# One layer of a hybrid streaming encoder: the adaLN modulation's products issued two loads at a time, in all four column groups

## The chip, the cores and the metric

One core of a Trainium2 chip runs the whole kernel. The metric is device time in microseconds of one execution. The core has a matrix engine (TensorE, PE; its weight loads are listed as PEld), a vector engine (VectorE, DVE), a scalar engine (ScalarE, ACT), GpSimd (POOL) and SyncE (SP), which issues most of the DMAs. Matrix results go to PSUM, everything else lies in SBUF.

## The reference, cut to what matters

Two groups of tokens (256 of a prompt, 32 of a sample, 288 in all) go through one layer of width 2048. Each of the two sequences has a vector c, and the layer begins with the modulation:

```python
(shift1, scale1, gate1, shift2, scale2, gate2) = silu(c) @ w_mod[l] + b_mod[l]
h = RMSNorm(x) * (1 + scale1) + shift1
P = h @ w_in[l]
...
x = x + gate1 * (merged @ w_out[l])
x = x + gate2 * SqReLU_MLP(RMSNorm(x) * (1 + scale2) + shift2)
```

w_mod is 2048 x 12288 in float32: six parts of 2048 columns, 16.8 MB each. Between h and merged lie three mixers (a gated recurrence, a state-space scan, a gated token mix); w_in, w_branch, w_out, w_up and w_down are the other large weights. All of it is read once from memory and has only 288 tokens (2 columns, for the modulation) to work on.

## The kernel before, in words

**Large products** (`product`, `product_part`, `product_group`). Weights arrive in tiles `raw` of 128 x 1024 float32 (512 KB), are split into a high and a low half by ACT (`whi`, L395) and DVE (`wlo`, L396), and three float32r matmuls of 288 columns for each 128 x 128 block add up the product (L382 to L384 in the first products, L413 to L415 later). There are six `raw` buffers, three `whi` and three `wlo`.

**The modulation.** silu(c) of the two sequences, padded to 32 columns, is the stationary operand `cT` (128 x 32 per block k of the contraction, 16 blocks). The moving operand is a block of w_mod. As the stationary operand has 32 columns only, a product fills one of the four 32-column groups of the array; its output goes to rows 32 cg to 32 cg + 31 of the PSUM tile `modps`, where cg is the group. The tiles of w_mod share the six `raw` buffers with the other weights.

Three generators make it, and `mods` chains them; one `next` is a step, which is one load and what follows it:
- `mod_stream` (L234 to L256) makes parts 0 and 1 (shift1, scale1), which the first products need. Units are 256 columns (the first eight) or 512 (the last four). A load has nk = 4 blocks of 256 columns or nk = 2 blocks of 512; block k goes to group k % 4, so a load of 256 columns has one product for each of the four groups, and a load of 512 columns has products for two of them. A product is the matmul at L246. After the last load of a unit, ACT copies the PSUM tile (L251), and `mod_flush` adds up the four groups with a selector (L317).
- `mod_parts` (L292 to L307) makes part 2 (gate1) in halves of 1024 columns. A load is one block k of 1024 columns, cut into four quarters of 256 columns, one for each group (L298).
- `mod_part_ve` makes parts 4, 3 and 5 on the vector engine; it isn't touched.

**The order.** The first products go through the contraction in the six parts `KG`, because h becomes known block by block; the loop over `KG` calls `mod_steps` 1.5 times for each weight tile (`MODR`) until parts 0 and 1 are done, and then 0.2 times (`RS`). In `product_group` the rate `mod_rate` is 0.2 at first and 0.4 from branch A on. Instructions are written in this order and a planner at build time, which runs a model of the time, arranges each engine's queue by priority: `tc.high_priority(offset=PRIO)` moves an instruction up by 2500 places, as is done with all loads and casts. The matmuls of the modulation have their ordinary place. The hardware then runs each queue in its order, with waits on semaphores; a buffer is taken again when all that read it are done.

Of the kernel before, what the change touches and what calls it, by code (L numbers as in the profile page):

```python
# [16 lines left out]
P = 128  # L17
D = 2048
NB = D // P            # blocks of the model width
SEQ, DEC = 256, 32  # L20
T = SEQ + DEC          # prompt tokens, then sample tokens
TX = T + 2             # and the shift of each sequence
# [4 lines left out]
CVB = 12               # blocks of the conv channels  # L27
# [9 lines left out]
def tile_step(ctx, tc, io, outs):  # L37
    nc = tc.nc
    V, S, G, TE = nc.vector, nc.scalar, nc.gpsimd, nc.tensor
# [7 lines left out]
    PRIO = 2500  # L47
    # the later parts of the modulation in their order, and those summed on the vector engine
    MOD_PARTS = (2, 4, 3, 5)
    MOD_VE = (4, 3, 5)  # L50
    # modulation steps per weight tile: in the first products, before, in and after branch A, in branch B,
    # in the output projection, in the MLP
    MODR, RS, RA, RB, RD, RW, RC = 1.5, 0.2, 0.4, 0.3, 0.5, 0.5, 0.25
    # buffers
    RAW, WHI, WLO = 6, 3, 3
    MTAG = ("raw", RAW)
    EVB = 6
    BLK = 34
    TMPB = 10
    # column pairs by which a branch's gates run ahead of its outputs  # L60
# [35 lines left out]
    # ------------------------------------------------------------------  # L96
    # constants
    # ------------------------------------------------------------------
# [7 lines left out]
    # triangular mask [s, t]: 1 where s <= t  # L106
# [3 lines left out]
    # scan resets at the chunk starts  # L110
# [4 lines left out]
    # selector that adds the four column groups of the modulation products  # L115
# [7 lines left out]
    def level_mask(pool, L):  # L123
        """mask [s, t] of the pairs that level L joins: one L-block, s in its first half, t in its second."""
        m = t1("lvm")
        if L == 1:
            V.tensor_copy(out=m, in_=ident)
        else:
            h = L // 2
            n = P // L  # L130
            G.memset(m, 1.0)
            if n > 1:
                G.affine_select(out=m, in_=m, pattern=[[-L, n], [0, L]], compare_op=ALU.is_ge,
                                fill=0.0, base=0, channel_multiplier=1)
            G.affine_select(out=m, in_=m, pattern=[[L, n], [0, L]] if n > 1 else [[0, L]], compare_op=ALU.is_ge,
                            fill=0.0, base=h - 1, channel_multiplier=-1)
            G.affine_select(out=m, in_=m, pattern=[[0, n], [1, L]] if n > 1 else [[1, L]], compare_op=ALU.is_ge,
                            fill=0.0, base=-h, channel_multiplier=0)
        # its 32-blocks next to each other
        mc = t1("lvm")[:, 0:32]  # L140
        V.tensor_reduce(out=mc, in_=m.rearrange("p (g t) -> p t g", g=4), axis=mybir.AxisListType.X, op=ALU.add)
        mu = pool.tile([P, 32], U8, name=f"lvm{L}")
        V.tensor_copy(out=mu, in_=mc)
        lv_masks[L] = mu

    # ------------------------------------------------------------------
    # parameters: rows to columns
    # ------------------------------------------------------------------
    # silu(c), feature-major, padded with zero columns
# [6 lines left out]
    with tc.high_priority(offset=2 * PRIO):  # L156
        ps = aux()
# [4 lines left out]
    # ones in one column of a sequence  # L162
# [5 lines left out]
    # x token-major, three blocks at a time (the sample's two)  # L168
# [59 lines left out]
    # ------------------------------------------------------------------  # L228
    # modulation: silu(c) @ w_mod + b_mod, as [feature, part*16+block, sequence]
    # ------------------------------------------------------------------  # L230
# [3 lines left out]
    def mod_stream(units):  # L234
        """256 or 512 columns at a time; a step is one load and its products."""
        for u, (c0, w) in enumerate(units):
            ps = paux.tile([P, 512], F32, tag="modps", name=nm("modps"), bufs=2)
            nk = 1024 // w
            for q in range(NB // nk):
# [3 lines left out]
                for i in range(nk):  # L243
                    k = nk * q + i
                    cg = k % 4
                    TE.matmul(ps[32 * cg:32 * cg + 32, 0:w], cT[:, k, :], raw[:, i, :],  # L246
                              start=k < 4, stop=k >= 12)
# [9 lines left out]

    def mod_part_ve(part):
        """A part in quarters of 512 columns, summed on the vector engine but for the sum over the partitions;
        a step is two blocks of the contraction."""  # L260
# [22 lines left out]
    def mod_parts(parts):  # L283
        """A part in halves of 1024 columns, a quarter of them in each group of 32 rows; a step is one block
        of the contraction."""
        for part in parts:
# [3 lines left out]
            for half in range(2):  # L290
                ps = paux.tile([P, 512], F32, tag="modps", name=nm("modps"), bufs=2)
                c0 = part * D + half * 1024  # L292
                for k in range(NB):
                    with tc.high_priority(offset=PRIO):
                        raw = wpool.tile([P, 1024], F32, tag=MTAG[0], name=nm("mraw"), bufs=MTAG[1])
                        nc.sync.dma_start(out=raw, in_=wm[:, k, c0:c0 + 1024])
                    for cg in range(4):
                        TE.matmul(ps[32 * cg:32 * cg + 32, 0:256], cT[:, k, :], raw[:, cg * 256:(cg + 1) * 256],  # L298
                                  start=k == 0, stop=k == NB - 1)
                    if k == 1:  # L300
                        mod_flush()
                    yield
# [8 lines left out]
    def mod_flush():  # L311
        """To feature-major, and adds the bias."""
# [26 lines left out]
    # the first products go through the contraction in these parts, as the modulation arrives  # L339
# [11 lines left out]
    def mod_drain(last):  # L351
        """All of the modulation up to a part."""
# [4 lines left out]
    # ------------------------------------------------------------------  # L357
    # streamed products: out^T[f, t] = sum_d w[d, f] a[d, t], three float32r passes
    # ------------------------------------------------------------------
    def product(w2d, col0, ncols, ahi, alo, evac, row0=0, n=T):  # L360
        """Groups of 256 columns; evac(j, psum) for each 128-column block."""
# [8 lines left out]
    def product_part(wv, cols, k0, nk, ahi, alo, accs, first):  # L370
        """nk blocks of the sum over d for sets of 256 columns, added to accs."""
# [50 lines left out]
    # ------------------------------------------------------------------  # L422
    # x feature-major, rms statistics, h = rmsnorm(x) (1 + scale1) + shift1
    # ------------------------------------------------------------------
# [55 lines left out]
    # ------------------------------------------------------------------  # L480
    # mixers
    # ------------------------------------------------------------------
# [3 lines left out]
    def setup_a():  # L486
# [3 lines left out]
        # lower bound of the forget gate: cumsum(softmax) - first, over the depth axis (one layer)  # L490
# [14 lines left out]
    bA, kA, qA, gA, vA = {}, {}, {}, {}, {}  # L505

    def evac_f(h0, pts):
        """log f, its running sum, and 1 - f of two heads; exponentials and logarithms from one table set."""
# [25 lines left out]
    def to_tokens(dst, src):  # L534
        """[feature, token] to [token, chunk, feature]."""
# [22 lines left out]
    def mixer_a(h):  # L558
# [4 lines left out]
        for L in (1, 2, 4, 8, 16, 32, 64, 128):  # L563
# [33 lines left out]
            # the joined pairs are whole squares  # L597
# [36 lines left out]
        # per-head rms norm  # L634
# [8 lines left out]
    def inv_rms(sq, scale):  # L643
        """1 / sqrt(scale * (sum of sq over its partitions) + eps), on all partitions."""
# [56 lines left out]
    def pair_rows(out, j, rows):  # L701
        """Rows 2 j and 2 j + 1 of a [16, n] tile, each on 64 partitions."""
# [4 lines left out]
    # time steps  # L707
# [18 lines left out]
    def do_dt():  # L726
# [26 lines left out]
        # token-major: [token, chunk, (dt | acum | dt * decay)]  # L753
# [8 lines left out]
        # exp(acum_last) on all partitions, for the second prompt chunk and the sample  # L762
# [7 lines left out]
        # acum in three parts of f32r each, 32 rows apart, and a selector that adds a head's three  # L770
# [16 lines left out]
    def mixer_b_cb(g):  # L787
        """C B^T of a group, causal, as [s, t]; B token-major."""
# [12 lines left out]
    def mixer_b(j):  # L801
        """Heads 2 j and 2 j + 1."""
# [10 lines left out]
        # x * dt and x * dt * decay, token-major  # L813
# [78 lines left out]
    def branch(kk, first, y, last=False):  # L892
        """gate_k * (y_k @ w_branch_k), added up; a step is 256 columns of it."""
# [101 lines left out]
    # ------------------------------------------------------------------  # L995
    # order of the work
    # ------------------------------------------------------------------
# [62 lines left out]
    # the last three tokens of each sequence are the new conv states  # L1060
# [14 lines left out]
    # The shift goes through the product in columns of its own, and 1 / rms comes after the product.  # L1075
# [55 lines left out]
    def final(j):  # L1131
        """Block j of the output: its squares, and times final_g."""
# [8 lines left out]
    def turn(j):  # L1141
        """Block j token-major."""
# [112 lines left out]
```

## Time and profile before

| | |
|---|---|
| device time, median of 3 runs | 2113.21 us (2109.93 to 2116.8) |
| the profiled execution: its span, which is the time the profile has for it | 2112.9 us |
| PE busy | 2079.8 us (98%) |
| PEld busy | 1966.6 us (93%) |
| DVE, ACT, POOL busy | 1442.7, 985.7, 156.6 us |
| read and written in memory | 405.04 MB, 4.62 MB |

The profile has one execution. An instruction is listed with the line that issued it, its engine and what it writes and reads (`out<-in`); groups of equal instructions are listed with their count, busy time and mean. A matmul's end is modelled and matmuls overlap, so what PE needs for a piece of work is read from start to start. A float32 matmul shows as two records, a float32r matmul as one. The chain of work that ended last is PE for 96% of the span.

### The profile page before, as it was taken

To read this page: it belongs to the slowest core of one execution; us is meant where nothing else is said; L and a number is where in the kernel's file an instruction comes from. 1 tells how busy PE (TensorE), PEld (TensorE's weight loads), DVE (VectorE), ACT (ScalarE), POOL (GpSimd) and SP (SyncE) were. 2 spreads that over 40 slices of the span, in tenths; PEclk is the share of its full clock that TensorE was granted. 3 is DMA by queue.
4 is the path that set the end of the run, shared out by engine and by line. 5 is a ranking of instruction groups with operands and counts; after the bars stand their busy time and mean duration, and the time that the engine had idled before them with its cause. 6 is when DMAs were issued, how large, how long until landed. Compare 5 with 4: busy or idle time off the path is not lost.

```text
span 2112.9 us, 40517 instructions
## 1 busy us (share of the span) xinstructions
PE 2079.8 (98%) x16336; PEld 1966.6 (93%) x16336; DVE 1442.7 (68%) x2546; ACT 985.7 (47%) x1553; POOL 156.6 (7%) x278
## 2 busy tenths in 40 slices
PE   6999999999999999999999999999999999999997
PEld 4777998988999999999999999999999999999997
DVE  2565666756578887787988998766774455555565
ACT  4432584655555545545444445433453344334443
POOL 2020112000000110110100110000000000000010
PEclk9999999999999999999999999999999999999999
DMA  9987655456566565666877777666664555555542
GB/s 295 295 263 238 217 150 163 144 183 179 181 204 196 172 192 183 191 183 182 268 245 221 221 226 229 201 206 203 199 210 160 169 160 166 164 169 161 167 156 91
DMA packets 364844, 412.31 MB, mean 195 GB/s; under 512 B 14777, under 2 KB 325457, under 8 KB 364657
## 3 DMA queue, kind: packets, MB, share of 16 engines
q1 hardware_dynamic: 360784, 403.97, 61.3%
q0 software_dynamic: 3008, 4.58, 0.7%
q8 instruction: 128, 2.10, 0.4%
q10 hardware_dynamic: 864, 1.18, 0.2%
q14 instruction: 60, 0.48, 0.1%
HBM read 405.04 MB, written 4.62 MB: 194 GB/s over the span
## 4 chain that ended last, share of the span: by engine, by line
PE 96%; DVE 1%; ACT 1%; DMA 1%; POOL 0%; issue 0%; SPq 0%; POOLq 0%; ACTq 0%; DVEq 0%
PE mm L413 26%; PE mm L415 26%; PE mm L414 26%; PE mm L382 3%; PE mm L383 3%; PE mm L384 3%; PE modps L246 2%; PE modps L298 1%; PE aux L185 1%; PE aux L856 1%; PE aux L584 1%; PE modps L317 0%; PE aux L538 0%; PE modps L328 0%; PE aux L631 0%; PE aux L601 0%
## 5 line engine op out<-in xcount | busy, mean ns | idle before, releaser
L395 ACT CAST whi<-raw 128x1024 fp32r<-128x1024 f32 x568 | 595.4, 1049 | 911.3 <-PE mm L414 701.5
L396 DVE TENSOR_TENSOR wlo<-raw,whi 128x1024 fp32r<-128x1024 f32 x568 | 695.0, 1224 | 453.8 <-ACT whi L395 451.2
L413 PE MATMUL mm<-hlo,whi 128*128 128x288 f32 x1408 | 421.3, 300 | 0.0
L414 PE MATMUL mm<-hhi,whi 128*128 128x288 f32 x1408 | 419.2, 299 | 0.0
L415 PE MATMUL mm<-hhi,wlo 128*128 128x288 f32 x1408 | 413.2, 299 | 0.0
L414 PE MATMUL mm<-h2hi,whi 128*128 128x290 f32 x1024 | 303.9, 297 | 0.0
L413 PE MATMUL mm<-h2lo,whi 128*128 128x290 f32 x1024 | 303.5, 297 | 0.0
L415 PE MATMUL mm<-uhi,wlo 128*128 128x288 f32 x1024 | 303.3, 296 | 0.0
L415 PE MATMUL mm<-h2hi,wlo 128*128 128x290 f32 x1024 | 302.8, 297 | 0.0
L413 PE MATMUL mm<-ulo,whi 128*128 128x288 f32 x1024 | 301.2, 294 | 0.0
L414 PE MATMUL mm<-uhi,whi 128*128 128x288 f32 x1024 | 301.1, 294 | 0.0
L274 DVE SCALAR_TENSOR_TENSOR macc<-mraw,cT,macc 128x512 f32<-128x512 f32 x360 | 259.2, 745 | 24.5 <-DMA mraw<-in_w_mod_dram 24.2
L413 PEld LDWEIGHTS mm<-hlo,whi 128*128 128x128 f32 x1408 | 265.5, 189 | 9.1 <-issue 6.8
L414 PEld LDWEIGHTS mm<-hhi,whi 128*128 128x128 f32 x1408 | 265.8, 189 | 2.4 <-issue 0.9
L415 PEld LDWEIGHTS mm<-hhi,wlo 128*128 128x128 f32 x1408 | 263.3, 189 | 3.3 <-issue 1.0
L413 PEld LDWEIGHTS mm<-h2lo,whi 128*128 128x128 f32 x1024 | 194.0, 189 | 0.5 <-ACT r L1162 0.2
L415 PEld LDWEIGHTS mm<-h2hi,wlo 128*128 128x128 f32 x1024 | 193.9, 190 | 0.2 <-issue 0.2
L414 PEld LDWEIGHTS mm<-h2hi,whi 128*128 128x128 f32 x1024 | 193.9, 189 | 0.1
L413 PEld LDWEIGHTS mm<-ulo,whi 128*128 128x128 f32 x1024 | 193.0, 188 | 0.4 <-issue 0.4
L414 PEld LDWEIGHTS mm<-uhi,whi 128*128 128x128 f32 x1024 | 192.6, 188 | 0.0
L415 PEld LDWEIGHTS mm<-uhi,wlo 128*128 128x128 f32 x1024 | 192.2, 188 | 0.1
L382 PE MATMUL mm<-hlo,whi 128*128 128x288 f32 x448 | 138.6, 309 | 0.4 <-DVE hlo L472 0.4
(398 smaller groups left out, 3085.4 us busy)
## 6 DMA issues: line engine op xcount, KB each, us to landing
raw<-in_w_in_dram SPq DMA_DIRECT2D x204, 512.0 KB, 3.9
mraw<-in_w_mod_dram SPq DMA_DIRECT2D x128, 512.0 KB, 4.1
raw<-in_w_up_dram SPq DMA_DIRECT2D x128, 512.0 KB, 3.8
raw<-in_w_down_dram SPq DMA_DIRECT2D x128, 512.0 KB, 3.4
raw<-in_w_mod_dram SPq DMA_DIRECT2D x64, 512.0 KB, 5.0
raw<-in_w_branch_dram SPq DMA_DIRECT2D x48, 512.0 KB, 4.2
raw<-in_w_out_dram SPq DMA_DIRECT2D x32, 512.0 KB, 4.6
raw<-in_w_in_dram SPq DMA_DIRECT2D x56, 256.0 KB, 4.7
```

What stands on the lines that cost most here:

```text
L185: TE.transpose(ps[:, t0:t0 + n], xrow[c, i][:, k * P:(k + 1) * P], ident[0:n, 0:n])
L246: TE.matmul(ps[32 * cg:32 * cg + 32, 0:w], cT[:, k, :], raw[:, i, :], start=k < 4, stop=k >= 12)
L274: V.scalar_tensor_tensor(out=acc[s], in0=raw[:, i], scalar=cs, in1=acc[s], op0=ALU.mult, op1=ALU.add)
L298: TE.matmul(ps[32 * cg:32 * cg + 32, 0:256], cT[:, k, :], raw[:, cg * 256:(cg + 1) * 256], start=k == 0, stop=k == NB - 1)
L382: TE.matmul(pt, whi[:, i, cs], alo[k], start=i == 0, stop=False)
L383: TE.matmul(pt, whi[:, i, cs], ahi[k], start=False, stop=False)
L384: TE.matmul(pt, wlo[:, i, cs], ahi[k], start=False, stop=i == nk - 1)
L395: S.copy(out=whi, in_=raw)
L396: V.tensor_sub(out=wlo, in0=raw, in1=whi)
L413: TE.matmul(pts[b], whi[:, i, cs], alo[k], start=k == 0, stop=False)
L414: TE.matmul(pts[b], whi[:, i, cs], ahi[k], start=False, stop=False)
L415: TE.matmul(pts[b], wlo[:, i, cs], ahi[k], start=False, stop=k == nk - 1)
```

## The change

Products of the modulation aren't issued at each load any more. `mod_stream` keeps them in `held` and issues them at every second load, with a new function `mod_cols`: for 512 columns that is four products, one for each group, and for 256 columns eight products, two for each group. `mod_parts` does the same with `MODB = 2` loads, eight products. The newest load's products go first (`reversed`), so that the first instruction waits for the later load; the others are made to follow it in PE's queue by `together`, which puts an edge from the first product to each of the others and raises their priority. `start` and `stop` (the first and the last product that adds to a PSUM region) follow the new order. All else in the diff is comments that are left out and line numbers that move.

```diff
+    MODB = 2
...
     def mod_stream(units):
         for u, (c0, w) in enumerate(units):
             ps = paux.tile([P, 512], F32, tag="modps", name=nm("modps"), bufs=2)
             nk = 1024 // w
+            held = []
             for q in range(NB // nk):
                 with tc.high_priority(offset=PRIO):
                     raw = wpool.tile([P, nk, w], F32, tag="raw", name=nm("raw"), bufs=RAW)
                     nc.sync.dma_start(out=raw, in_=wm[:, nk * q:nk * (q + 1), c0:c0 + w])
-                for i in range(nk):
-                    k = nk * q + i
-                    cg = k % 4
-                    TE.matmul(ps[32 * cg:32 * cg + 32, 0:w], cT[:, k, :], raw[:, i, :],
-                              start=k < 4, stop=k >= 12)
+                held += [(nk * q + i, raw[:, i, :]) for i in range(nk)]
+                if q % 2:
+                    mod_cols(ps, held, w)
+                    held = []
...
+    def together(works):
+        first = works[0]()
+        with tc.issue_after(first.ins), tc.high_priority(offset=PRIO):
+            for work in works[1:]:
+                work()
+
+    def mod_cols(ps, held, w):
+        works, begun = [], set()
+        for k, r in reversed(held):
+            cg = k % 4
+            works.append(partial(TE.matmul, ps[32 * cg:32 * cg + 32, 0:w], cT[:, k, :], r,
+                                 start=held[0][0] == 0 and cg not in begun, stop=k == held[0][0] + cg and held[-1][0] == NB - 1))
+            begun.add(cg)
+        together(works)
...
     def mod_parts(parts):
...
+                held = []
                 for k in range(NB):
                     with tc.high_priority(offset=PRIO):
                         raw = wpool.tile([P, 1024], F32, tag=MTAG[0], name=nm("mraw"), bufs=MTAG[1])
                         nc.sync.dma_start(out=raw, in_=wm[:, k, c0:c0 + 1024])
-                    for cg in range(4):
-                        TE.matmul(ps[32 * cg:32 * cg + 32, 0:256], cT[:, k, :], raw[:, cg * 256:(cg + 1) * 256],
-                                  start=k == 0, stop=k == NB - 1)
+                    held.append((k, raw))
+                    if len(held) == MODB:
+                        together([partial(TE.matmul, ps[32 * cg:32 * cg + 32, 0:256], cT[:, k1, :],
+                                          r[:, cg * 256:(cg + 1) * 256], start=k < MODB and k1 == k,
+                                          stop=k == NB - 1 and k1 == held[0][0])
+                                  for k1, r in reversed(held) for cg in range(4)])
+                        held = []
```

## Rows read from the trace of the kernel before

**Rows 1.** The page, busy time of each engine.
```profile
PE 2079.8 (98%) x16336; PEld 1966.6 (93%) x16336; DVE 1442.7 (68%) x2546; ACT 985.7 (47%) x1553; POOL 156.6 (7%) x278
```

**Rows 2.** The page, busy tenths of PE in 40 equal slices.
```profile
PE   6999999999999999999999999999999999999997
```

**Rows 3.** Busy time by stretch: instructions in brackets, granted clock, DMA share, GB/s.
```profile
12.00:40.00 28.00, 22.93 (x140) 12.66 (x132) 7.05 (x17) 13.28 (x44) 6.60 (x20) 1.00 1.05 352
40.00:105.00 65.00, 65.00 (x529) 51.60 (x528) 34.96 (x63) 29.73 (x55) 0.00 (x0) 1.00 0.89 283
105.00:222.00 117.00, 117.00 (x788) 88.47 (x788) 71.02 (x151) 34.62 (x46) 11.88 (x21) 1.00 0.80 253
222.00:620.00 398.00, 393.43 (x3510) 359.75 (x3507) 264.21 (x596) 231.61 (x380) 45.96 (x88) 0.99 0.58 173
```

**Rows 4.** Timeline of PE around one visit: start, busy, instruction, records.
```profile
233.34 0.30 PE L383 MATMUL mm<-hhi,whi 128*128 128x288 f32 x1
233.48 0.29 PE L384 MATMUL mm<-hhi,wlo 128*128 128x288 f32 x1
233.70 0.64 PE L298 MATMUL modps<-mraw,cT 128*32 128x256 f32 x8
234.27 0.40 PE L382 MATMUL mm<-hlo,whi 128*128 128x288 f32 x1
234.51 0.30 PE L383 MATMUL mm<-hhi,whi 128*128 128x288 f32 x1
```

**Rows 5.** Timeline of PE, three visits of other sizes.
```profile
84.48 1.07 PE L246 MATMUL modps<-raw,cT 128*32 128x256 f32 x16
...
104.79 1.05 PE L246 MATMUL modps<-raw,cT 128*32 128x512 f32 x2
...
114.24 1.06 PE L246 MATMUL modps<-raw,cT 128*32 128x512 f32 x8
```

**Rows 6.** Timeline of PEld, the weight loads of the visit at 114.24.
```profile
114.24 0.16 PEld L246 LDWEIGHTS modps<-raw,cT 128*32 128x32 f32 x8 [0.16 <-issue]
```

**Rows 7.** Groups by shape on PE, 40 to 222 us: records, busy us, mean ns.
```profile
L246 PE MATMUL modps<-raw,cT 128*32 128x512 f32 x128 | 30.1, 604 | 0.0
L246 PE MATMUL modps<-raw,cT 128*32 128x256 f32 x168 | 15.0, 388 | 0.0
```

**Rows 8.** Timeline of PE, the first and last visits of each kind.
```profile
40.84 0.64 PE L246 MATMUL modps<-raw,cT 128*32 128x256 f32 x8
...
102.64 1.06 PE L246 MATMUL modps<-raw,cT 128*32 128x256 f32 x6
...
217.04 0.62 PE L246 MATMUL modps<-raw,cT 128*32 128x512 f32 x2
217.05 0.63 PE L298 MATMUL modps<-mraw,cT 128*32 128x256 f32 x4
...
607.90 0.64 PE L298 MATMUL modps<-mraw,cT 128*32 128x256 f32 x8
```

**Rows 9.** Groups by shape on PE, 217 to 620 us.
```profile
L298 PE MATMUL modps<-mraw,cT 128*32 128x256 f32 x256 | 23.8, 400 | 1.7 <-DMA mraw<-in_w_mod_dram 1.7
```

**Rows 10.** Timeline of PE at the start, two visits of L246.
```profile
18.61 1.08 PE L246 MATMUL modps<-raw,cT 128*32 128x256 f32 x8 [0.56 <-DMA raw<-in_w_mod_dram]
...
27.79 1.94 PE L246 MATMUL modps<-raw,cT 128*32 128x256 f32 x16
```

**Rows 11.** Waits before L246 (us, times): whole span first, then two of 40 to 222.
```profile
  DMA raw<-in_w_mod_dram: 12.4, 7
...
  issue: 6.6, 37
  PE mm L383: 0.3, 2
```

**Rows 12.** Modulation loads on the page (KB, us to landing); ACT's wait, 40 to 222.
```profile
raw<-in_w_mod_dram SPq DMA_DIRECT2D x64, 512.0 KB, 5.0
...
ACT whi L395 <- DMA raw<-in_w_in_dram: 35.2, 10, 6.0
```

More of the change, by code (lines that the diff above doesn't have):

```diff
@@ L1 @@
 from contextlib import ExitStack
+from functools import partial
 from itertools import chain
```

## The prediction

> **What bounds the kernel now.** I read the page's busy times first. TensorE (PE) is busy 98% of the span [rows 1], and its line of slices shows the one hole, in the first slice [rows 2]. The table by stretch says the same where the change acts: PE is busy 65.00 of 65.00 us from 40 to 105, 117.00 of 117.00 from 105 to 222, and 393.43 of 398.00 from 222 to 620 [rows 3]. A busy PE can still be slow, so I looked at single starts in the timeline: ordinary matmuls follow each other at 0.13 to 0.14 us (233.34 to 233.48 in [rows 4]), without holes. So from 40 us on, a microsecond that PE no longer needs comes off the end, as long as the loads keep up. They nearly don't: the DMA share is 0.89 and then 0.80 in the first two stretches, where the modulation's weights arrive, and only 0.58 after [rows 3].
>
> **How a modulation visit is priced.** Each fp32 product shows as two matmul records. I call a run of modulation records between other matmuls a visit. Around the visit at 233.70 [rows 4] the matmul before starts at 233.48 and the second one after at 234.51: 1.03 us in which two ordinary spacings would have used 0.27. The visit costs 0.76 us where its row shows 0.64 busy, so cost is busy time plus 0.12.
>
> The records then show what a visit's length depends on [rows 5]:
> - two records of 512 columns (one product, one column group): busy 1.05;
> - eight records of 512 columns (four products, four groups): busy 1.06;
> - eight of 256 columns (four groups, once): 0.64 [rows 4];
> - sixteen of 256 columns (four groups, twice): 1.07.
>
> So products in different groups share one pass over the array, a second pass of 256 columns costs 0.43, and a visit costs some 0.2 by itself plus 0.12 at its neighbours. Both forms that the change makes, four groups of 512 columns and two passes of 256, already occur, so nothing in the sum needs a new price.
>
> The weight loads don't spoil this: eight of them take 0.16 us together, at the start of the visit [rows 6]. The Trainium skill (TensorE: Matmul & The Clock Gate, Part 3, "The mechanism") says that weight loads overlap running matmuls only where the row group differs; here all products use all rows, so by that rule the four groups would take turns. By this trace they do not. What the rule would make of the time is the fourth rival.
>
> **The change part by part.** No load, copy or flush is added or removed; each load is issued at the step where it was. The products of an even step are kept and go out behind those of the odd step. The visits are fewer.
>
> (a) *512-column units.* Before: 128 records, 30.1 us busy [rows 7], in 27 visits, from the mixed one at 102.64 to the mixed one at 217.04 [rows 8], because a load holds two of the four groups only. Cost 30.1 + 27 x 0.12 = 33.3. After: 64 products, four a visit, 16 visits of 1.06 + 0.12: 18.9. Saved 14.4 us.
>
> (b) *256-column units, from 40 us on.* Before: 168 records, 15.0 busy [rows 7], in 19 visits, 40.84 to 102.64 [rows 8]: 15.0 + 19 x 0.12 = 17.3. After: 10.5 visits of sixteen, each 1.07 + 0.12: 12.5. Saved 4.8 us at most. Here the DMA share is highest, so this gain may only uncover loads. I take half, 2.4; the bounds are 0 and 4.8.
>
> (c) *Part 2 (the gate of the mixers).* Before: 256 records, 23.8 busy [rows 9], in 36 visits, 217.04 to 607.90 [rows 8] (a few are split in two or three): 23.8 + 36 x 0.12 = 28.1. After: 16 visits of 1.19: 19.0. Saved 9.1 us, in a stretch with DMA to spare.
>
> The two mixed visits [rows 8] stand in two groups each and their records overlap, so each is counted once too often, at some 0.6 to 0.7 busy and 0.12: 1.6 us off.
>
> (d) *The start.* Before 38 us PE waits for loads and matmuls run at half the later rate: eight records are busy 1.08, sixteen 1.94 [rows 10], against 0.64 and 1.07 later. (The clock column reads 1.00 there; the durations say 1.2 GHz, not 2.4.) A unit's last visit starts when its last load has landed and now holds two passes: 1.94 - 1.08 = 0.86 us later for what waits on it. Two raw buffers instead of one are held meanwhile. Against that, a pair saves 2 x 1.08 - 1.94 = 0.2 where PE is the limit. I take a loss of 1.0; bounds from a gain of 0.5 (two or three pairs) to a loss of 3 (three times 0.86, and half a microsecond of loads).
>
> (e) *The wait that is added.* The visit's first product now waits for the later of two loads. PE takes its queue in order, so the product groups behind it wait too, and through them the buffers whi and wlo, the casts, and the raw buffers. From 40 to 222 us PE waits for no modulation load at all: the only waits before those lines are 6.6 us of issue in 37 pieces and two for a matmul [rows 11]. The cover is the six raw buffers, loaded ahead. I cost the wait at nothing beyond the half of (b); its price without cover is the third rival.
>
> (f) *The raw buffer held a step longer.* A held load keeps one of six. From 40 to 105 us a load of 0.52 MB is used every 1.85 us (65 us x 283 GB/s is 18.4 MB, 35 loads). Six buffers give 11.1 us from one use to the next; landing takes 5.0 [rows 12]; a hold across one weight tile costs 24 x 0.133 plus a visit, 4.3 us, for one load in three. That leaves about 1.8 us: thin, but on one buffer, not on all. The next thing late would be the cast that waits for raw, where ACT already waits 35.2 us in ten pieces [rows 12] without PE feeling it. After 222 us the hold is longer, five weight tiles at a rate of 0.2, but the load rate is 173 GB/s, and five buffers are then left for 3.2 us tiles.
>
> **Sum.** 14.4 + 2.4 + 9.1 - 1.6 - 1.0 = 23.3 us off the profiled execution's span of 2112.9, which is 0.3 below the median of the runs shown: 2089.6, and 2090 as a median.
>
> **Rivals.**
> 1. *The forecast*, as above; from 2084 to 2097 with (b) at either end, the bounds of (d), and a re-planned order of the rest worth some 3 us (the runs shown differ by that from their median). Chance 0.65.
>
> 2. *The loads set the pace up to 222 us.* 40 to 222 us moves 18.4 + 29.6 = 48.0 MB. If PE gives up 19 us there, 163 are left, which asks for 294 GB/s. The rows show 283 where the share is 0.89, and 352 from 12 to 40 us at a share of 1.05 [rows 3]. Against this rival: 352 covers it. For it: with thinner buffering 283 may be all there is, and then 48.0 MB take 170 us. With (b) gone and half of (a), the saving is 7.2 + 9.1 - 1.6 - 1.0 = 13.7, 2099.5 us; with all of (a) gone it is 6.5, 2106.7. Chance 0.17.
>
> 3. *Slower: PE stands at the pair's second load.* Where: the 26.5 visits between 40 and 222 us. Price: when PE waits for a modulation load at the start, it waits 12.4 us in 7 pieces, 1.8 each [rows 11]. If each visit did so, 47 us would be lost and 23.3 gained: about 2137. It decides from 23.3 / 26.5 = 0.9 us a visit. For it: the margin of 1.8 us in (f). Against: PE loses nothing to these loads there now [rows 11]. Chance 0.07.
>
> 4. *The groups take turns in the 512-column visits.* Then (a) saves only the visits' own 0.33 us, 11 of them, 3.6 instead of 14.4: 2101. The eight records in 1.06 us [rows 5] speak against it. (This is what the rule of the Trainium skill named above would give.) Chance 0.02.
>
> 5. *It doesn't do what it says.* The first product keeps its place in the planned order and the others follow by an edge and a raised priority. If other work still lands between them, or the planner, with new lifetimes of the buffers, moves weight tiles later by as much, the visits stay as many: 2113, give or take 5. Chance 0.09.
>
> **How the numbers follow.** A measurement of this kernel can tell about 0.3%, 6.3 us, from no change, so faster means under 2106.9. Faster: 0.65, 0.12 of rival 2 and 0.02 of rival 4: 0.79. Same: the rest of rival 2 and rival 5, 0.14. Slower: 0.07. The range 2083 to 2107 holds the forecast, nearly all of rival 2, and rival 4: about 0.82. Both its ends come from the cases; its lower end is the sum with all of (b) and a gain at the start, 27.2, plus 3 for the order.
>
> **What would show it.** In the changed kernel's timeline the 512-column visits should hold eight records and be busy 1.06, 16 of them; the 256-column visits sixteen records at 1.07, about 10 after 40 us and 16 of part 2. The groups by line should fall from 30.1, 15.0 and 23.8 us busy to about 17, 11 and 17. The last visit of the streamed units should move from 217 us to about 200, and that of part 2 from 608 to about 585; from there to the end nothing should change. The forecast is wrong if visits before 222 us show idle time ended by a load of the modulation or by a cast (rivals 2 and 3), if the records of a pair are not adjacent (5), or if the stretch after 610 us grows.

## The result, and the profile after

The changed kernel takes 2087.42 us (median of 4 runs, 2087.02 to 2088.34) against 2112.71 for the kernel before (4 runs, 2109.93 to 2116.8): a ratio of 0.9882, 95% interval 0.9868 to 0.9896. The forecast was 2090, from 2083 to 2107. The profiled execution's span is 2086.6 us, 26.3 less than before; its own time is 2088.34. As in every run here that has both, the span is 1.7 us below the time; by that the 2112.9 of before belongs to an execution of about 2114.6, slower than its median.

The stretches that answer to [rows 3], in the changed kernel (busy time by stretch: PE, PEld, DVE, ACT, POOL, granted clock, DMA share, GB/s):

```profile
40.00:105.00 65.00, 65.00 (x567) 55.45 (x560) 38.69 (x75) 32.40 (x59) 0.00 (x0) 1.00 0.93 304
105.00:222.00 117.00, 115.73 (x880) 97.74 (x879) 78.95 (x164) 40.60 (x55) 11.40 (x21) 1.00 0.84 273
222.00:620.00 398.00, 394.40 (x3588) 367.25 (x3587) 273.44 (x624) 246.05 (x402) 48.26 (x98) 1.00 0.58 175
```

PE is still the limit, but more gets through it: from 105 to 222 us it starts 880 matmul records where it started 788. The loads went along, at 304 GB/s where there were 283. From 105 to 222 us PE is idle for 1.27 us, which it wasn't.

A 512-column visit of the changed kernel, in PE's timeline, to be set beside the row at 104.79 in [rows 5]. L264 is the first product of `together`, L267 the others:

```profile
105.02 0.29 PE L410 MATMUL mm<-hhi,wlo 128*128 128x288 f32 x1
105.25 0.62 PE L264 MATMUL modps<-raw,cT 128*32 128x512 f32 x1
105.25 0.63 PE L267 MATMUL modps<-raw,cT 128*32 128x512 f32 x3
105.70 0.59 PE L264 MATMUL modps<-raw,cT 128*32 128x512 f32 x1
105.71 0.60 PE L267 MATMUL modps<-raw,cT 128*32 128x512 f32 x3
106.24 0.40 PE L408 MATMUL mm<-hlo,whi 128*128 128x288 f32 x1
106.48 0.29 PE L409 MATMUL mm<-hhi,whi 128*128 128x288 f32 x1
```

Eight records, from 105.25 to 106.24: 0.99 us for four products, the time that two records alone took before. The spacings beside it are 0.23 and 0.24 us, as the price of a visit had them. All visits look so: I count 47 runs of such records in the trace instead of 86, the 512-column ones of eight records and the others of sixteen (the very first holds two pairs).

Busy time of what reads `cT` (the modulation's products), by stretch, PE first; the kernel before:

```profile
40.00:105.00 65.00, 15.68 (x173) 4.78 (x174) 0.00 (x0) 0.00 (x0) 1.00 0.89 283
105.00:222.00 117.00, 29.48 (x134) 4.49 (x134) 0.00 (x0) 0.00 (x0) 1.00 0.80 253
222.00:620.00 398.00, 22.42 (x248) 5.41 (x244) 5.00 (x8) 0.00 (x0) 0.99 0.58 173
```

and the changed one (after PE and PEld comes DVE, whose entries belong to the parts that it sums, and ACT):

```profile
40.00:105.00 65.00, 12.29 (x180) 4.36 (x172) 0.00 (x0) 0.00 (x0) 1.00 0.93 304
105.00:222.00 117.00, 17.05 (x136) 2.78 (x136) 0.00 (x0) 0.00 (x0) 1.00 0.84 273
222.00:620.00 398.00, 16.06 (x240) 6.26 (x240) 10.66 (x16) 0.00 (x0) 1.00 0.58 175
```

67.6 us of PE have become 45.4 for as many records: 22.2 less. After 38 us the visits are 43 instead of 80, and 37 times 0.12 at their neighbours is 4.4 more: 26.6, against 26.3 between the two spans. That these are so close is in part luck: the two spans also differ by 1.7 us at the start, by PE's waits, and by stretches at the lower clock (below).

To see where on the way the time was gained, I numbered the 13632 matmuls of the large products, which are the same in all these kernels, and compared when the n-th starts. "Earlier" is against the trace of before, in us; the three kernels to the right belong to the next section.

| n-th matmul | before starts at | the change, earlier | 512 columns alone | 256 alone | part 2 alone |
|---|---|---|---|---|---|
| first | 34.8 | 1.7 | 0.6 | 0.6 | 0.5 |
| 340 | 104.3 | 5.9 | 0.8 | 4.8 | 1.3 |
| 900 | 220.0 | 17.6 | 13.3 | 4.5 | 1.7 |
| 2800 | 552.1 | 25.5 | 18.1 | 9.1 | 9.5 |
| last | 2099.0 | 26.3 | 16.4 | 9.0 | 11.6 |

From the first to the 900th, each column gains where its own units are and, within some 1 us, nowhere else. Behind that, up to the 2800th, the two kernels whose part 2 is the old one gain another 4 to 5 us. Some 4 of them come between 315 and 370 us, where the granted clock falls to its lower level twice in the trace of before, behind waits of PE of 2.3 and 1.7 us, and never in theirs:

```profile
328.80:332.20 3.40, 3.40 (x20) 2.32 (x18) 3.37 (x6) 1.05 (x1) 0.00 (x0) 0.50 0.24 85
362.90:366.30 3.40, 3.40 (x21) 3.14 (x14) 0.22 (x1) 0.31 (x1) 0.00 (x0) 0.50 0.53 157
```

So every column has this trait of one trace in it, and I take places from the traces and sizes from the medians.

### The profile page after: what moved, and what is told of

The parts are those of the page before. It is cut to its first block, busy times and chain, and to the rows that moved or that the text cites. A ratio compares the mean times of both kernels' runs of the same rounds, so it can differ in the third digit from the quotient of the medians.

```text
span 2086.6 us, 40501 instructions
## 1 busy us (share of the span) xinstructions
PE 2053.2 (98%) x16336; PEld 1963.7 (94%) x16336; DVE 1442.1 (69%) x2546; ACT 992.4 (48%) x1558; POOL 165.8 (8%) x278
## 4 chain that ended last, share of the span: by engine, by line
PE 93%; DMA 3%; DVE 1%; ACT 1%; POOL 0%; issue 0%; SPq 0%; ACTq 0%; POOLq 0%; DVEq 0%
PE mm L439 26%; PE mm L441 26%; PE mm L440 26%; PE mm L408 3%; PE mm L410 2%; PE mm L409 2%; DMA raw<-in_w_mod_dram 1%; PE modps L264 1%; DMA raw<-in_w_in_dram 1%; PE modps L267 1%; PE aux L882 1%; PE aux L188 1%; PE aux L610 1%; DVE wlo L422 0%; PE aux L564 0%; PE modps L354 0%
## 5 line engine op out<-in xcount | busy, mean ns | idle before, releaser
L295 DVE SCALAR_TENSOR_TENSOR macc<-mraw,cT,macc 128x512 f32<-128x512 f32 x360 | 259.3, 746 | 21.4 <-DMA mraw<-in_w_mod_dram 21.2
```

Of the source, the lines that this page charges most:

```text
L295: V.scalar_tensor_tensor(out=acc[s], in0=raw[:, i], scalar=cs, in1=acc[s], op0=ALU.mult, op1=ALU.add)
```

## The experiments

**Each part alone.** Three kernels in which one of the three places is changed and the other two issue their products load by load, in the old order. In the stream that is, for the first of them:

```diff
-                if q % 2:
+                if w == 256:
+                    for k, r in held:
+                        cg = k % 4
+                        TE.matmul(ps[32 * cg:32 * cg + 32, 0:w], cT[:, k, :], r, start=k < 4, stop=k >= 12)
+                    held = []
+                elif q % 2:
                     mod_cols(ps, held, w)
                     held = []
```

> Only the 512-column units are paired; the 256-column units and part 2 are issued load by load, as before. Theory (a visit costs its passes and some 0.33 us, and four groups share a pass): 14.4 us less than before, 2098 (2095 to 2102). Rival (the loads set the pace up to 222 us): 7 us less or fewer, 2105 or more. Rival (what pays is the number of visits alone): 11 visits of 0.33 us, 3.6 less, 2109.

> Only the 256-column units are paired. Theory: 8.5 visits fewer after 40 us at some 0.5 us with their splits, 4.8 less at most and about 2 at the start as the trace after shows: 2107 (2104 to 2111). Rival (loads set the pace there): 2112, no change.

> Only part 2 is paired. Theory: 20 visits fewer and fewer passes, 9.1 less by the prediction's sum, 7 by the shift between the traces: 2104 (2102 to 2107). Together with the two kernels beside it the savings add up to 25 if the parts are independent.

Measured on one chip, where the kernel before had 2110.95 (15 runs): 512 columns alone 2098.4, ratio 0.9938 (0.9925 to 0.995), 12.5 us less; 256 alone 2106.05, 0.998 (0.9971 to 0.9989), 4.9 less; part 2 alone 2102.27, 0.9958 (0.9945 to 0.997), 8.7 less. The sum is 26.1, and all three at once gave 25.3: as far as intervals of 2 to 3 us to either side can tell, the parts add up. The rival of loads that set the pace falls. It gave the 256-column units nothing, and they gave 4.9 (2.3 to 6.1); the start is in this number too, but in the trace 4.2 us are gained between the first large matmul and the 340th, where the DMA share is highest.

**Four groups, or fewer visits?** Both changed together. This kernel takes the loads of a 512-column unit in another order, so that a pair holds the same two groups: equal loads, equal visits.

```diff
-            for q in range(NB // nk):
+            for n, q in enumerate((0, 2, 1, 3, 4, 6, 5, 7) if w == 512 else range(NB // nk)):
...
-                if q % 2:
+                if n % 2:
```

> The change, but in the 512-column units the loads come in another order, so that the two that are paired hold the same two column groups. Same loads, same products, same 16 visits of four products. Theory (what pays is four groups in one pass): a visit has two passes of 0.85 us instead of one, busy 1.9 instead of 1.06, 16 x 0.85 = 13.6 us more than the change: 2101 (2098 to 2104). Rival (what pays is fewer visits): 2087, as the change.

2097.24 us (2094.85 to 2099.36), 9.8 more than the change. In its timeline such a visit is:

```profile
106.14 0.29 PE L420 MATMUL mm<-hhi,wlo 128*128 128x288 f32 x1
106.36 0.62 PE L274 MATMUL modps<-raw,cT 128*32 128x512 f32 x1
106.37 0.62 PE L277 MATMUL modps<-raw,cT 128*32 128x512 f32 x1
106.82 0.59 PE L274 MATMUL modps<-raw,cT 128*32 128x512 f32 x1
106.82 1.45 PE L277 MATMUL modps<-raw,cT 128*32 128x512 f32 x5
108.20 0.44 PE L188 MATMUL aux<-ident,xt 128*128 128x128 f32 x2
```

The same eight records last from 106.36 to 108.20, 1.84 us instead of 0.99: two passes. Sixteen times 0.85 is 13.6, and at the 900th matmul this trace is 13.2 us behind the change's. By the end it is 11.1 behind; where the other 2 went was not looked into. So of the 12.5 us that the 512-column units give, 9.8 are the groups'. The 2.7 that are left are near what 11 visits fewer are worth at 0.33 us (3.6); with intervals of some 3 us that share isn't shown.

**The order within a visit.** I expected PE to start matmuls in the order of its queue, so that two products of one group side by side would block it.

```diff
-        for k, r in reversed(held):
+        for k, r in sorted(reversed(held), key=lambda kr: -(kr[0] % 4)):
...
-                                  for k1, r in reversed(held) for cg in range(4)])
+                                  for cg in range(4) for k1, r in reversed(held)])
```

> The change, but inside the 256-column visits and those of part 2 the two products of one group stand next to each other instead of one round over the four groups after another. Same products, same visits. If PE starts its matmuls in queue order, a visit has five passes instead of two, 3 x 0.43 = 1.3 us more in each of 27 visits after 40 us: 35 more than the change, 2122. If groups start on their own, or if only the number of visits pays: 2087, as the change.

2085.74 us (2084.66 to 2086.74), ratio 0.988: no loss. A visit of part 2, whose queue now has the two products of one group one behind the other:

```profile
231.98 0.29 PE L410 MATMUL mm<-hhi,wlo 128*128 128x288 f32 x1
232.20 0.40 PE L264 MATMUL modps<-mraw,cT 128*32 128x256 f32 x1
232.22 0.43 PE L267 MATMUL modps<-mraw,cT 128*32 128x256 f32 x3
232.44 0.38 PE L264 MATMUL modps<-mraw,cT 128*32 128x256 f32 x1
232.46 0.84 PE L267 MATMUL modps<-mraw,cT 128*32 128x256 f32 x11
233.22 0.40 PE L408 MATMUL mm<-hlo,whi 128*128 128x288 f32 x1
```

It lasts from 232.20 to 233.22, 1.02 us. The change's, with the groups in rounds, lasts 1.00:

```profile
231.92 0.40 PE L264 MATMUL modps<-mraw,cT 128*32 128x256 f32 x1
...
232.92 0.40 PE L408 MATMUL mm<-hlo,whi 128*128 128x288 f32 x1
```

In the kernel with the new order three more records start within 0.04 us of the first, and the first product's own second record only at 232.44: products of other groups pass those whose group is busy. My reading of the queue was wrong; the price of a visit doesn't depend on it.

**More loads kept, and fewer or more buffers.** Four loads instead of two in all three places (`q % 4 == 3`, `MODB = 4`); in part 2 alone (`MODB = 4`); the change, and the kernel before, with five raw buffers (`RAW = 5`); the change, and the kernel with four loads in part 2, with seven (`RAW = 7`, and for the room `TMPB = 9`, one buffer for temporaries less).

> Four loads are kept instead of two, in all three places. Theory: 21 visits fewer, 0.33 us each, 7 us less than the change, 2080, if the loads keep up. Rival (the held raw buffers): four of the six buffers are kept for a visit, two are left for loads that take 5.6 us to land, and PE waits up to 222 us for what is loaded: some 1 us or more for each visit there, 2090 to 2110, with idle time of PE ended by loads or casts in that stretch.

2097.1 us (2094.21 to 2101.91): the visits are 24, and yet it is 9.7 slower than the change. Its stretches:

```profile
40.00:105.00 65.00, 60.35 (x508) 52.62 (x508) 31.55 (x59) 26.55 (x52) 0.00 (x0) 0.95 0.82 263
105.00:222.00 117.00, 111.84 (x860) 94.70 (x860) 74.50 (x162) 40.01 (x57) 11.02 (x21) 0.99 0.84 276
```

PE is idle for 4.7 and 5.2 us, and the loads come at 263 GB/s instead of 304 from 40 to 105 us: held buffers throttle the loads. But PE doesn't stand at the modulation's loads, as the third rival has it. From 40 to 222 us it waits 0.3 us for them, and 7.2 for the copies and additions into `acc` that free the PSUM tiles of the large products. The longest of these waits (engines PE, ACT and DVE alone):

```profile
85.36 1.04 ACT L421 CAST whi<-raw 128x1024 fp32r<-128x1024 f32 x1 [6.47 <-DMA raw<-in_w_in_dram]
...
86.44 1.23 DVE L422 TENSOR_TENSOR wlo<-raw,whi 128x1024 fp32r<-128x1024 f32 x1 [3.84 <-ACT whi L421]
87.58 0.45 DVE L416 TENSOR_TENSOR acc<-acc,mm 128x288 f32<-128x288 f32 x1
...
88.08 0.61 PE L408 MATMUL mm<-hlo,whi 128*128 128x288 f32 x1 [2.66 <-DVE acc L416]
```

A load of the other weights is late, ACT's cast waits for it, DVE's part of the split for the cast, the addition comes behind that on DVE, and PE waits for the addition. This is the late cast of the prediction's (f). Late in this wait, and behind one of 2.2 us that begins at 149, the granted clock falls to 0.50, from 87.4 to 94.2 and from 152.2 to 155.6; half of these 10.2 us, an estimated 5 at most, comes on top.

> Four loads are kept in part 2 alone, whose stretch has DMA to spare. Theory: 8 visits of 0.33 us fewer, 2.6 less than the change: 2085 (2083 to 2086). If three held buffers leave too few for the weight tiles: 2088 or more.

> Four loads kept in part 2, with seven raw buffers and nine temporaries. If the held buffers made four loads slower than two (2091.8 against 2087.4), a seventh buffer gives most of it back: 2085 to 2088. If it is the order (a visit that fills no hole of PE any more, as the trace shows 2.4 us of waiting for POOL at 309 us and 1.9 for DVE at 554), it stays at 2090 to 2093.

With six buffers 2091.78 us (0.9909, 0.9893 to 0.9926), slower than with two loads kept; with seven 2084.93 (0.9881, 0.9864 to 0.9897). One explanation was PE's waits in the mixers. The trace with six buffers has these, from 222 to 620 us (waits of PE: us, times, longest):

```profile
PE aux L672 <- POOL ssC L997: 2.4, 1, 2.4
PE aux L784 <- DVE dt L771: 2.1, 1, 2.1
PE aux L627 <- DVE att L629: 1.9, 1, 1.9
```

The first two are in the trace with seven buffers as well, and that one is no slower than the change: most of the loss came back with the seventh buffer, or with the plan that comes with it. But beside the kernel with seven buffers and two loads kept (below, 2084.68) four loads gain nothing, where 8 visits fewer should give 2.6 us. From 222 to 620 us, four loads first, then two:

```profile
222.00:620.00 398.00, 390.98 (x3580) 367.00 (x3579) 273.69 (x620) 247.35 (x397) 52.87 (x97) 0.99 0.56 179
222.00:620.00 398.00, 395.39 (x3610) 368.13 (x3610) 277.42 (x633) 247.24 (x403) 47.89 (x97) 1.00 0.56 176
```

PE is idle for 7.0 us with four and for 2.6 with two; the wait for POOL is in the first trace alone. The gain may go into such waits, but that rests on single traces and isn't shown.

> The change with five raw buffers instead of six. By the prediction's margin (1.8 us left of 11.1 with six), a buffer less takes 1.85 us and leaves nothing: PE waits a little at some of the pairs up to 222 us, 2089 to 2097. If the buffers have more room than that sum says: 2087. If the pairs live on the sixth buffer alone: over 2100.

> The kernel before with five raw buffers. The change with five lost 8 us. If pairing is what needs the sixth buffer (a held load takes one away), the kernel before loses clearly less, 0 to 3 us: 2112 to 2115. If the sixth buffer is as much needed without pairs, it loses 8 too: 2120.

The change with five buffers takes 2095.4 us (2092.83 to 2096.82), 8 more; in its trace PE is idle for 0.9 and 4.0 us in the two stretches up to 222 us. I expected the kernel before to need the sixth less; it loses 16: 2126.87, ratio 1.0082 (1.0067 to 1.0097). Half of that shows in what reads `cT`, in that kernel:

```profile
40.00:105.00 65.00, 16.84 (x162) 4.89 (x162) 0.00 (x0) 0.00 (x0) 0.99 0.83 263
105.00:222.00 117.00, 31.98 (x132) 4.57 (x130) 0.00 (x0) 0.00 (x0) 1.00 0.75 241
222.00:620.00 398.00, 25.23 (x254) 6.02 (x252) 0.00 (x0) 0.00 (x0) 1.00 0.56 173
```

Its visits are 97 instead of 86, and busy 74.1 us instead of 67.6. Without `together`, the plan has more and shorter visits with five buffers; PE shows no idle time up to 222 us (65.00 of 65.00 and 117.00 of 117.00), it works longer. The changed kernel keeps its 47 visits with five buffers. That accounts for some 8 of the 16 us (6.5 busy and 11 visits at 0.12), and the trace is 7.8 behind that of before at the 800th large matmul, at 202 us. The rest comes behind 480 us and was not taken apart.

> The change with seven raw buffers; room for it is made by nine instead of ten buffers for temporaries. The trace of the change shows PE idle for 1.3 us between 105 and 222 us, before visits that wait for a load. If that is all the pairs cost, 1 to 2 us less than the change: 2085 to 2087; if the tenth temporary is needed by the mixers, some us more. Below 2084 would mean that the held buffers cost more than the idle time shows.

2084.68 us (2083.73 to 2085.29), ratio 0.988 (0.9865 to 0.9895). PE's idle time from 105 to 222 us is gone in its trace (117.00 of 117.00), but by ratio this kernel can't be told from the change.

**The two lowest together.**

> The two variants of the change that came out lowest, together: products of one group next to each other (2085.7) and seven raw buffers with nine temporaries (2084.7). If the two gains of 2 to 3 us against 2087.4 were real and separate, 2082 to 2084; if they are the planner's luck, 2084 to 2088, not to be told from the change.

2085.89 us (2084.63 to 2086.3), ratio 0.9882 (0.9862 to 0.9902). The gains don't add up; none of these is shown to beat the change.

## Why the prediction was right, point by point

- *PE is the limit, and what it no longer does comes off the end.* Right: 22.2 us less busy with the modulation and 25.3 less at the end. The visits are as foretold, the last streamed one at 199.45 us and the last of part 2 at 590.56, where I had about 200 and 585.
- *The price of a visit* (busy plus 0.12, passes of 0.43 for 256 columns) held in the visits looked at: from a visit's start to the next matmul 0.99 for four groups of 512, 1.00 for sixteen records of 256, 1.84 where two groups take two passes. The Trainium skill (FP8 and Floating Point Precision, "TensorE Precision Notes") gives true fp32 four passes through the array. By that, 4 x 256 columns at 2.4 GHz are an estimated 0.43 us, which agrees with the 0.43 of these traces.
- *(a) 14.4 us:* 12.5 measured alone (10.6 to 15.8 by its interval). *(c) 9.1:* 8.7 (6.3 to 11.6).
- *(b), of which I took half, 2.4:* this term was mis-sized. With the start in it, the 256-column units alone gave 4.9 (2.3 to 6.1), and 4.2 behind the start in the trace, near the upper bound of 4.8. I had asked whether the loads could follow and found 294 GB/s needed; they came at 304 from 40 to 105 us.
- *(d), a loss of 1.0 at the start:* not seen. The first product's matmul starts 1.7 us earlier in the change's trace. But 256 alone, which has the pairs there, starts 0.6 earlier, and so do 512 alone (0.6) and part 2 alone (0.5), whose start is the old one. So whether the pairs gain anything at the start is open.
- *The sum, 2.6 us too slow:* for (b) and (d) together I had 1.4 us, and the kernel with both gave 4.9. For (a) and (c), less 1.6 for the mixed visits, I had 21.9, and they gave 21.2. So the second error hides a little of the first, which is luck.
- *(e), the added wait, at nothing:* nearly. PE's waits from 40 to 222 us are

```profile
PE modps L264 <- DMA raw<-in_w_mod_dram: 1.1, 2, 0.6
PE mm L410 <- DVE wlo L422: 0.2, 1, 0.2
```

  1.1 us in two pieces in front of visits, against the 0.9 us a visit from which the third rival decides. Its price was read too high: the 12.4 us in 7 pieces of [rows 11] add up the waits of PE and of PEld. PE alone waits 5.9 us in 4 pieces, 1.5 each, and so 39 us instead of 47 would have been lost.
- *(f), thin cover:* right in that one buffer less costs the change 8 us, and holding four loads 9.7, where its late cast is what the trace shows. Wrong in the thought that the pairs are what uses it up: the kernel before, without pairs, loses 16 with five buffers.
- *The rule on row groups (rival 4):* the trace of the change has the four first records of a visit start within 0.02 us of each other, with all rows in use, as [rows 6] already told. The Trainium skill (TensorE: Matmul & The Clock Gate, Part 3, "The mechanism") also has matmuls start strictly in queue order. The kernel with the order changed within a visit speaks against that between column groups, and the measurement decides.

## What to carry to other kernels

When a stationary operand fills 32 columns only, count passes and visits: products in all four column groups cost one pass, and by the spacings in these traces a trip from full-array work and back costs some 0.3 us by itself. So collect until the four groups are full and the trips are few. Fix the adjacency in the queue instead of leaving it to the planner: the old order went from 86 to 97 visits with a buffer less, the new one kept its 47. What `together` does without the pairs was not tested. Stop collecting where the held input buffers begin to throttle the loads: two loads of six buffers paid here, four did not, and four in part 2 alone brought nothing even with seven.

## What was not expected of the hardware

PE doesn't hold back a product of a free column group behind one whose group is busy: sixteen records took 1.02 us with each group's two products adjacent in the queue, and 1.00 with the groups in rounds. And PE's rate at the start differs between traces: after PE has worked with hardly a gap since 20.6 us, the large matmuls run at 0.24 us apiece, the lower of the two clock levels, up to 38.6 us in the trace of before. In the changed kernel's, behind an idle time of 1.3 us, the first starts at 33.13, two follow at the full rate, and from 33.63 to 36.98 they are at 0.24 again (its granted clock from 12 to 40 us reads 0.94). The trace of before, then the changed kernel's:

```profile
38.37 0.42 PE L384 MATMUL mm<-hhi,wlo 128*128 128x288 f32 x1
38.61 0.32 PE L382 MATMUL mm<-hlo,whi 128*128 128x288 f32 x1
38.76 0.29 PE L383 MATMUL mm<-hhi,whi 128*128 128x288 f32 x1
```

```profile
33.50 0.33 PE L410 MATMUL mm<-hhi,wlo 128*128 128x288 f32 x1
33.63 0.43 PE L408 MATMUL mm<-hlo,whi 128*128 128x288 f32 x1
33.87 0.44 PE L409 MATMUL mm<-hhi,whi 128*128 128x288 f32 x1
...
36.98 0.33 PE L410 MATMUL mm<-hhi,wlo 128*128 128x288 f32 x1
37.16 0.29 PE L408 MATMUL mm<-hlo,whi 128*128 128x288 f32 x1
```

In the thirteen other traces the higher level comes to stay, for the stretch up to 50 us, between 34.4 and 41.0 us, and in that of part 2 alone, which has the old products there, at 36.3; so it isn't the change's doing alone, and 1 us there says little.
